# Second MLP product by one level of Strassen, with the sums of its weight blocks made by DMAs in HBM

## The chip, the cores and the metric

The kernel runs on one core of a Trainium2 chip. The metric is the device time of one execution in microseconds (us); lower is better. One execution was recorded by the hardware profiler; its rows are quoted below.

## What is computed

The kernel is a decoder layer for 512 tokens of width 1024: a gated merge of a convolution branch and an attention branch, a cross-attention to 256 memory tokens, a squared-ReLU MLP of width 4096, and a final norm. The change lies in the MLP:

```python
u = rms_norm(h, norm_mlp_g[l])                                      # [512, 1024]
h = h + jnp.square(jax.nn.relu(u @ w_mlp1[l])) @ w_mlp2[l]          # [1024, 4096], [4096, 1024]
return rms_norm(h, final_norm_g)
```

All is float32. The kernel makes each float32 product from three passes over operands that are split into a high and a low part.

## The kernel before

Activations lie feature-major, [feature, token]. A *unit* is one output tile: eight 128-row blocks of weights against 512 tokens, three passes each (`mm3`: high x high, high x low, low x high), so 24 matmuls of 128x512. The TensorE (PE) queue is in the order of emission; the queues of the other engines are put in order by a scheduler when the program is built, which may place an instruction earlier than the line that emits it if nothing holds it there.

Weights come from HBM as chunks of at most 1 MB into `raw` (two buffers, loads on SP's queue). `prep` splits a unit's part of a chunk: ScalarE (ACT) casts it into `wh`, and another engine subtracts to get `wl` (three buffers each). That other engine is `w_eng`: VectorE (DVE) for the first units, then GpSimd (POOL) from the third convolution tile on, through the input products, attention, merge and most of the cross-attention, and DVE again from `w_eng[0] = dve` just ahead of the MLP. `Pipe` emits a unit's split ahead of the products of the unit before it.

The MLP goes by halves of the hidden features. `m1_unit` makes one tile of the first product, `evac_m1` scales it by the row factors, squares and splits it into `hh` and `hl_`; then `m2_unit` multiplies the 16 tiles of the half by eight column tiles of `w_mlp2` and adds into the residual `ht`. That is 768 matmuls of 128x512 for the first product and 768 for the second. The last output tile goes by token halves, with the final norm of the first half beside the products of the second (`last_*`).

Of the kernel before, what the change touches and what calls it, by code (L numbers as in the profile page):

```python
# [23 lines left out]
P = 128  # L24
# [68 lines left out]
# gate chunks that come before the key/value latents  # L93
# [3 lines left out]
def _stream():  # L97
    """The weight chunks in the order of use: key, matrix, first row, row blocks, columns."""
# [34 lines left out]
    for h in range(2):  # L133
        for i in range(8):
            out.append((("m1", h, i), "w_mlp1", 0, 8, r(2048 * h + 256 * i, 256)))
        for i in range(8):
            out.append((("m2", h, i), "w_mlp2", 16 * h, 16, r(128 * i, 128)))
    return out


def _pack(arrays):
    """All weight chunks, each [partition, row block, column], one after the other."""
    parts = []
    for _, name, k0, kt, cols in _stream():
        w = arrays[name][0][k0 * P:(k0 + kt) * P]
# [20 lines left out]
def _body(tc, a):  # L166
# [30 lines left out]
    # ---------------------------------------------------------------- exact splits and products  # L197
# [8 lines left out]
    # PE issues in the order of emission; small products that wait for other engines are put off  # L206
    # by a number of ticks (a tick: three passes over 512 columns)
# [20 lines left out]
    def mm3(out, pairs, first=True, last=True):  # L228
        n = len(pairs)
        cols = out.shape[-1] / S  # L230
        for i, ((wh, wl), (ah, al)) in enumerate(pairs):
            pe.matmul(out, wh, ah, start=first and i == 0, stop=False)  # L232
            pe.matmul(out, wh, al, start=False, stop=False)  # L233
            pe.matmul(out, wl, ah, start=False, stop=last and i == n - 1)  # L234
            tick(cols)
# [11 lines left out]
    # ---------------------------------------------------------------- constants  # L247
# [31 lines left out]
    # ---------------------------------------------------------------- weight stream  # L279
    stream = _stream()  # L280
    ch, offs = {}, []
    o = 0
    for i, (key, _, _, kt, cols) in enumerate(stream):
        ch[key] = i
        offs.append(o)
        o += P * kt * len(cols)
    raws = {}
    issued = [0]
    RAW_BUFS = 2

    def raw(*key):
        ci = ch[key]
        while issued[0] < len(stream) and issued[0] < ci + RAW_BUFS:
# [4 lines left out]
            src = a["weights"][offs[i]:offs[i] + P * n].rearrange("(p n) -> p n", p=P)  # L298
# [27 lines left out]
    class Pipe:  # L326
        """splits the weights of one unit ahead of the unit before it."""
# [22 lines left out]
    # ================================================================ scopes of the first half  # L350
# [34 lines left out]
    # ---------------------------------------------------------------- x * g, split  # L385
    # the tables of the scalar engine and the clock of the PE array come up while the first loads run
# [34 lines left out]
    # ---------------------------------------------------------------- rotary tables  # L421
# [50 lines left out]
    # ---------------------------------------------------------------- background conv work  # L472
# [14 lines left out]
    def conv_gen():  # L487
        # two channel tiles in turn, so that no step waits for the one before it
# [16 lines left out]
    def layer_norm_in():  # L505
        # token-major
# [47 lines left out]
    # ---------------------------------------------------------------- w_in  # L554
# [41 lines left out]
    # first pair of channel tiles: both products follow the arriving row blocks of x  # L596
# [39 lines left out]
    # latent projections, token-major: [token, column]  # L636
# [94 lines left out]
    # ================================================================ MLA  # L731
# [148 lines left out]
    # ================================================================ merge and w_out  # L880
# [73 lines left out]
    class Norm:  # L954
        """h += psum; h * g, split; the sums of squares of h's rows."""

        def __init__(self, pl, gname, oh_, ol_):
# [18 lines left out]
        def sums(self):  # L976
            r = rstd_rows(self.acc, D)
            after(D_R2, lambda: self.bcast(r))
# [8 lines left out]
        def then(self, fn):  # L987
            """runs fn once the rows' factors are there."""
# [21 lines left out]
    for m in range(KD):  # L1010
        out_unit(m)
        if m == 2:
            mem_norm()
# [5 lines left out]
    # ================================================================ memory cross-attention  # L1019
# [97 lines left out]
    n2 = Norm(hgp, "norm_mlp_g", hgh, hgl)  # L1117
# [16 lines left out]
    pipe.ahead(lambda: prep(("m1", 0, 0)))  # L1134
    close(xa_cm, xm_cm)

    # ================================================================ MLP
    ml_cm, mlp = pool("mlp", side="right")
    hh = mlp.tile([P, 16, S], F32R, name="hh")
    hl_ = mlp.tile([P, 16, S], F32R, name="hl")  # L1140

    def evac_m1(b, m):
        t = mlp.tile([P, S], F32, tag="mz", name="mz", bufs=2)
        dve.scalar_tensor_tensor(t, b, 0.0, n2.rb, op0=ALU.max, op1=ALU.mult)  # L1144
        s = mlp.tile([P, S], F32, tag="ms", name="ms", bufs=2)
        act.activation(s, t, AF.Square)
        if m == 0:
            act.activation(warm, s[:, 0:1], AF.Sqrt)
        split(hh[:, m, :], hl_[:, m, :], s)

    def m1_unit(half, m):
        def main(hl):
            b = bank()
            mm3(b, hg_pairs(hl))
            n2.then(lambda: evac_m1(b, m))
        pipe.unit(lambda: prep(("m1", half, m // 2), c0=128 * (m % 2)), main)

    fin = mlp.tile([P, S], F32, name="fin")
    eps = mlp.tile([P, 1], F32, name="eps")
    gps.memset(eps, EPS)  # L1160
    mb_ = {}

    def m2_unit(half, m, q):
        def main(hl):
            if q == 0:
                mb_[0] = bank()
            b = mb_[0]
            mm3(b, [(lhs(hl, k), (hh[:, 8 * q + k, :], hl_[:, 8 * q + k, :])) for k in range(8)],
                first=q == 0, last=q == 1)
            if q == 1:  # L1170
                dve.tensor_tensor(ht[:, m, :], ht[:, m, :], b, op=ALU.add)
                if half == 1:
                    if m == 0:
                        act.activation(fin, ht[:, m, :], AF.Square)
                    else:
                        s = mlp.tile([P, S], F32, tag="ms", name="ms", bufs=2)
                        act.activation(s, ht[:, m, :], AF.Square)
                        dve.tensor_tensor(fin, fin, s, op=ALU.add)
                    act.activation(ht[:, m, :], ht[:, m, :], AF.Copy, scale=v_("final_norm_g", m))
        pipe.unit(lambda: prep(("m2", half, m), k0=8 * q, kt=8), main)  # L1180

    for half in range(2):
        for m in range(16):
            m1_unit(half, m)
        for m in range(KD - half):
            for q in range(2):
                m2_unit(half, m, q)
# [3 lines left out]
    m = KD - 1  # L1191
    lw = [prep(("m2", 1, m), k0=8 * q, kt=8) for q in range(2)]
    pipe.flush()
    HS = S // 2
    ydst = a["yT"].rearrange("(k p) t -> p k t", p=P)

    def last_mm(b, hf, i):
        """an eighth of the products of a token half."""
        sl = slice(hf * HS, hf * HS + HS)
        q, k0 = i // 4, 2 * (i % 4)  # L1200
        mm3(b[:, :HS], [(lhs(lw[q], k), (hh[:, 8 * q + k, sl], hl_[:, 8 * q + k, sl]))
                        for k in range(k0, k0 + 2)], first=i == 0, last=i == 7)

    def last_add(b, hf):
        """the sums of squares of a token half."""
        sl = slice(hf * HS, hf * HS + HS)
# [82 lines left out]
```

## Time and profile before

| what | value |
|---|---|
| time, median of 3 runs | 814.03 us (814.02 to 814.56) |
| span of the profiled execution, first to last instruction | 811.6 us |
| TensorE busy / weight load | 783.2 us (97%) / 647.3 us (80%) |
| VectorE / ScalarE / GpSimd busy | 495.9 us / 346.4 us / 158.6 us |
| mean granted TensorE clock | 0.989 |
| HBM read / written | 74.97 MB / 2.10 MB |

The profiled execution is read by its span; the median of the runs is 2.4 us above it, which is taken as what lies around the span. A busy PE means that a matmul is in flight, not that it is at its peak.

### The profile page before, as it was taken

How to read it: one execution, taken by the hardware profiler on the slowest of the kernel's cores; microseconds unless marked ns; L12 is line 12 of the kernel's file. 1: busy time of each engine (PE TensorE's matmuls, PEld its weight loads, DVE VectorE, ACT ScalarE, POOL GpSimd, SP SyncE). 2: the span in 40 equal slices, each digit the busy share in tenths (PEclk: the TensorE clock that was granted, in tenths of full speed). 3: DMA queues.
4: the chain of work that ended last, by engine and by line, in shares of the span. 5: the costliest groups of instructions: out<-in, count | busy, mean ns of one | idle time of the engine just before them, and what ended most of it. 6: DMA issues, size and time to landing. Idle time of an engine off the chain costs nothing.

```text
span 811.6 us, 9532 instructions
## 1 busy us (share of the span) xinstructions
PE 783.2 (97%) x3730; PEld 647.3 (80%) x3730; DVE 495.9 (61%) x781; ACT 346.4 (43%) x585; POOL 158.6 (20%) x92
## 2 busy tenths in 40 slices
PE   8799999999999998998999999999999999999995
PEld 4589788778788886888878888888888888888885
DVE  5898999734888869766787654443233444533333
ACT  7323334478666546343475354332212434432321
POOL 4444436322321304445320000000000000000001
PEclk9999999999999998999999999999999999999998
DMA  8213124122103242232321322222332222222203
GB/s 274 95 45 124 55 82 156 62 81 92 53 1 105 98 162 104 103 105 104 105 104 52 105 104 104 86 79 96 103 104 104 104 96 76 89 103 104 104 0 104
DMA packets 18492, 77.67 MB, mean 96 GB/s; under 512 B 1680, under 2 KB 7184, under 8 KB 11024
## 3 DMA queue, kind: packets, MB, share of 16 engines
q1 hardware_dynamic: 15120, 72.00, 25.6%
q10 hardware_dynamic: 3328, 5.07, 1.8%
q8 instruction: 29, 0.48, 0.2%
q14 instruction: 15, 0.12, 0.1%
HBM read 74.97 MB, written 2.10 MB: 95 GB/s over the span
## 4 chain that ended last, share of the span: by engine, by line
PE 75%; DVE 18%; ACT 3%; issue 3%; DMA 1%; SPq 0%; DVEq 0%; ACTq 0%
PE mm L234 23%; PE mm L232 23%; PE mm L233 23%; DVE cv L483 6%; DVE q L200 1%; DVE mt L906 1%; DVE rs_t L243 1%; DMA xr<-xT 1%; PE at L799 1%; DVE sg L710 1%; PE at L778 1%; PE at L780 1%; ACT wh L199 1%; PE at L781 0%; DVE mt L905 0%
## 5 line engine op out<-in xcount | busy, mean ns | idle before, releaser
L199 ACT CAST wh<-raw 128x1024 fp32r<-128x1024 f32 (+4 forms) x135 | 136.5, 1012 | 321.5 <-PE mm L233 279.7
L200 POOL TENSOR_TENSOR wl<-raw,wh 128x1024 fp32r<-128x1024 f32 (+4 forms) x65 | 144.6, 2227 | 255.2 <-ACT wh L199 248.1
L200 DVE TENSOR_TENSOR wl<-raw,wh 128x1024 fp32r<-128x1024 f32 x70 | 85.7, 1224 | 73.3 <-ACT wh L199 73.3
L232 PE MATMUL mm<-hgh,wh 128*128 128x512 f32 x288 | 113.0, 392 | 0.0
L234 PE MATMUL mm<-hgh,wl 128*128 128x512 f32 x288 | 112.8, 392 | 0.0
L233 PE MATMUL mm<-hgl,wh 128*128 128x512 f32 x288 | 112.6, 391 | 0.0
L232 PE MATMUL mm<-hh,wh 128*128 128x512 f32 (+1 forms) x272 | 102.6, 377 | 0.0
L233 PE MATMUL mm<-hl,wh 128*128 128x512 f32 (+1 forms) x272 | 102.4, 376 | 0.0
L234 PE MATMUL mm<-hh,wl 128*128 128x512 f32 (+1 forms) x272 | 102.4, 376 | 0.0
L483 DVE SCALAR_TENSOR_TENSOR cv<-zpad,vec,cv 128x512 f32<-128x512 f32 x116 | 80.0, 744 | 0.1
L1245 POOL TENSOR_TENSOR ht<-ht,rbf 128x256 f32<-128x256 f32 x4 | 2.9, 736 | 384.1 <-ACT rbf L1237 384.1
L232 PE MATMUL mm<-uh,wh 128*128 128x512 f32 x176 | 71.3, 405 | 1.8 <-DVE sg L710 1.8
L1144 DVE SCALAR_TENSOR_TENSOR mz<-mm,rb 128x512 f32<-128x512 f32 x32 | 22.0, 691 | 79.7 <-PE mm L234 78.7
L234 PE MATMUL mm<-uh,wl 128*128 128x512 f32 x176 | 69.8, 397 | 0.5 <-DVE wl L200 0.5
L233 PE MATMUL mm<-ul,wh 128*128 128x512 f32 x176 | 69.9, 397 | 0.0
L234 PEld LDWEIGHTS mm<-hgh,wl 128*128 128x128 f32 x288 | 54.3, 189 | 11.5
L233 PEld LDWEIGHTS mm<-hgl,wh 128*128 128x128 f32 x288 | 54.5, 189 | 11.2
L232 PEld LDWEIGHTS mm<-hgh,wh 128*128 128x128 f32 x288 | 54.5, 189 | 11.2
L234 PEld LDWEIGHTS mm<-hh,wl 128*128 128x128 f32 x272 | 51.2, 188 | 9.4
L232 PEld LDWEIGHTS mm<-hh,wh 128*128 128x128 f32 x272 | 51.2, 188 | 9.4
L233 PEld LDWEIGHTS mm<-hl,wh 128*128 128x128 f32 x272 | 51.2, 188 | 9.3
L232 PEld LDWEIGHTS mm<-uh,wh 128*128 128x128 f32 x176 | 33.3, 189 | 11.1 <-issue 3.8
(327 smaller groups left out, 1407.1 us busy)
## 6 DMA issues: line engine op xcount, KB each, us to landing
raw<-weights SPq DMA_DIRECT2D x58, 1024.0 KB, 4.8
raw<-weights SPq DMA_DIRECT2D x4, 768.0 KB, 4.2
xr<-xT SPq DMA_DIRECT2D x8, 256.0 KB, 6.2
raw<-weights SPq DMA_DIRECT2D x4, 512.0 KB, 5.1
ht<-xT ACTq DMA_DIRECT2D x1, 2048.0 KB, 9.4
raw<-weights SPq DMA_DIRECT2D x2, 576.0 KB, 3.4
mr<-memT ACTq DMA_DIRECT2D x1, 1024.0 KB, 5.8
mtok<-mem ACTq DMA_DIRECT2D x1, 1024.0 KB, 7.9
```

Source lines behind the costliest of these rows:

```text
L199: act.copy(hi, src)
L200: (eng or dve).tensor_tensor(lo, src, hi.bitcast(F32), op=ALU.subtract)
L232: pe.matmul(out, wh, ah, start=first and i == 0, stop=False)
L233: pe.matmul(out, wh, al, start=False, stop=False)
L234: pe.matmul(out, wl, ah, start=False, stop=last and i == n - 1)
L243: dve.scalar_tensor_tensor(t, dst, -0.5, dst, op0=ALU.mult, op1=ALU.mult)
L483: dve.scalar_tensor_tensor(run if w < CW - 1 else acc[:, c, :], zs, wcol, run, op0=ALU.mult, op1=ALU.add)
L710: dve.tensor_tensor(t, b, rbx, op=ALU.mult)
L778: pe.matmul(b[:, :n], q[:, 0, sl], k[:, 0, :n], start=True, stop=False)
L780: pe.matmul(b[:, :n], q[:, 0, sl], k[:, 1, :n], start=False, stop=False)
L799: pe.transpose(b[:, (t - k) * P:(t - k + 1) * P], ptok[h, t][:, k * P:(k + 1) * P], ident)
L1144: dve.scalar_tensor_tensor(t, b, 0.0, n2.rb, op0=ALU.max, op1=ALU.mult)
```

## The change

The hidden activations A (512 tokens by 4096) and the weights B (4096 by 1024) of the second product are each cut into two by two blocks, and the eight block products become seven (Strassen-Winograd). The operands are A11, S1, S2, S4, S3, A12, A22 against B11, X, Y, B22, V, B21, Z, with

- S1 = A21 - A22 (kept as `s3 - a22`), S2 = A11 - S1 with the signs as in the code, S3, S4 likewise: four subtractions on DVE for each pair of hidden tiles, beside the first product;
- X = B12 + B11, V = B12 + B22, Y = B11 + V, Z = B21 + Y: made in HBM, by 16 plain copies of 1 MB and 16 accumulating DMAs of 1 MB, all on POOL's queue (`b_sums`).

The second product becomes token-major: the activations' blocks are the stationary operand, 512 weight columns the moving one. It runs as 7 passes of 4 chunks; a chunk is one 1 MB load, one split of 128x1024 of activations (`split_h`) and two of weights (`split_w`), and 24 matmuls. A chunk needs a load of its own, so the product takes 28 loads of 1 MB where it took 16. The row factors are applied when the sums leave PSUM; the residual is transposed by PE beside the first product and written to HBM (`spill`), and read back for each output tile. The final norm is token-major.

```diff
+    def b_sums_gen():
+        ...
+        start = lambda c: [(("x", c), b12(c)), (("v", c), b12(c)), (("y", c), b11(c)), (("z", c), b21(c))]
+        adds = lambda c: [(("x", c), b11(c)), (("v", c), b22(c)), (("y", c), sums["v", c]),
+                          (("z", c), sums["y", c])]
+        for c in range(4):
+            for d, s_ in start(c):
+                gps.dma_start(out=sums[d], in_=s_)
+                yield
+            if c > 0:
+                for d, s_ in adds(c - 1):
+                    gps.dma_start(out=sums[d], in_=s_, accum_op=ALU.add, max_dma_last_dim=8192)
+                    yield
+        for d, s_ in adds(3):
+            gps.dma_start(out=sums[d], in_=s_, accum_op=ALU.add, max_dma_last_dim=8192)
+            yield
...
     for m in range(KD):
         out_unit(m)
+        b_sums(1)
...
+    def m1_unit(p, j):
+        ...
+            act.activation(r, b, AF.Relu)
+            for half in range(2):
+                dst = block((("a11", "a12"), ("s3", "a22"))[half][j], c)[:, i]
+                act.activation(dst, r[:, half * HT:(half + 1) * HT], AF.Square)
+            if j == 1 and p % 2 == 1:
+                dve.tensor_tensor(s1, s3, a22, op=ALU.subtract)
+                dve.tensor_tensor(s3, s3, a11, op=ALU.subtract)
+                dve.tensor_tensor(s2, a11, s1, op=ALU.subtract)
+                dve.tensor_tensor(s4, a12, s2, op=ALU.subtract)
+    def spill(m):
+        for t in range(NT):
+            pe.transpose(b[:, t * P:(t + 1) * P], ht[:, m, t * P:(t + 1) * P], ident)
+        act.copy(t_.rearrange("p t c -> p (t c)"), b)
+        act.dma_start(out=hsp[:, m * P:(m + 1) * P].rearrange("(t p) c -> p t c", p=P), in_=t_)
+    for p in range(16):
+        for j in range(2):
+            m1_unit(p, j)
+        if 1 <= p <= KD:
+            spill(p - 1)
+        b_sums(2)
...
+    def split_h(name, c):
+        pl = m2w.get("p", mlp)
+        hi = pl.tile([P, 4, HT], F32R, tag="hA", name="hA", bufs=2 if pl is not mlp else 1)
+        lo = pl.tile([P, 4, HT], F32R, tag="hB", name="hB", bufs=2 if pl is not mlp else 1)
+    PASSES = (("a11", "b11", "a", False), ("s1", "x", "c", False), ("s2", "y", "b", False),
+              ("s4", "b22", "c", True), ("s3", "v", "b", True), ("a12", "b21", "a", True),
+              ("a22", "z", "b", True))
+    for n in range(len(PASSES)):
+        for c in range(4):
+            pass_unit(n, c)
```

Where the scheduler puts the DMAs is not seen in the diff. The first place is the beginning of POOL's queue. The names: `wl` is the low part of a weight split, `xr` and `nacc` are the sums of squares of the input, `x_0_80` is the block sum X of chunk 0 in HBM, `weights` the packed weights; a DMA's shape is rows by elements. Before:

```order
L416 MEMSET cs_106 128x4
L200 ISA
L200 TENSOR_TENSOR wl_165<-raw_135,wh_164 128x256 [waits DMAHW3_49,Activation_49]
L200 TENSOR_TENSOR wl_165<-raw_135,wh_164 128x512 [waits DMAHW5_49,Activation_49]
L200 TENSOR_TENSOR wl_167<-raw_135,wh_166 128x512 [waits DMAHW0_49,Activation_49]
L200 TENSOR_TENSOR wl_167<-raw_135,wh_166 128x512 [waits DMAHW3_49,Activation_49]
L568 TENSOR_TENSOR xr_85<-xr_85 128x512 [waits Activation_49]
L568 TENSOR_TENSOR xr_85<-xr_85 128x512 [waits Activation_49,Pool_49] x2
L569 TENSOR_TENSOR nacc_86<-xr_85 128x512 [waits DVE_49,Pool_49]
```

Now:

```order
L474 MEMSET cs_124 128x4
L333 DMA x_0_80<-weights 16x16384
L333 DMA v_0_84<-weights 16x16384
L227 ISA
L227 TENSOR_TENSOR wl_183<-raw_153,wh_182 128x256 [waits DMAHW3_49,Activation_49]
L227 TENSOR_TENSOR wl_183<-raw_153,wh_182 128x512 [waits DMAHW5_49,Activation_49]
L227 TENSOR_TENSOR wl_185<-raw_153,wh_184 128x512 [waits DMAHW0_49,Activation_49]
L227 TENSOR_TENSOR wl_185<-raw_153,wh_184 128x512 [waits DMAHW3_49,Activation_49]
L626 TENSOR_TENSOR xr_103<-xr_103 128x512 [waits Activation_49]
L333 DMA y_0_88<-weights 16x16384
L626 TENSOR_TENSOR xr_103<-xr_103 128x512 [waits Activation_49,Pool_49]
L333 DMA z_0_92<-weights 16x16384
```

The copies that the code emits beside the merge product and the first MLP product stand at the very start of the program, two of them ahead of the first weight split.

The second place is farther down the same queue, in the gate products of the input stage, where the last chain of adds stands (Y of chunk 3 waits for V, Z for Y; DMASW names the landing of an earlier DMA of POOL's). Before:

```order
L694 TENSOR_TENSOR krr_110<-krt_109 128x4x16
L696 COPY krr_110<-krr_110 128x4x64 [waits Pool_49]
L200 TENSOR_TENSOR wl_1200<-raw_1082,wh_1199 128x1024 [waits DMAHW4_49,PE_49,Activation_49]
L200 TENSOR_TENSOR wl_1238<-raw_1082,wh_1237 128x1024 [waits PE_49,Activation_49]
L200 TENSOR_TENSOR wl_1278<-raw_1197,wh_1277 128x1024 [waits DMAHW5_49,PE_49,Activation_49]
```

Now:

```order
L340 DMA y_3_91<-v_3_87 128x2048 [waits DMASW6_49,DMASW4_49]
...
L227 TENSOR_TENSOR wl_1218<-raw_1100,wh_1217 128x1024 [waits DMAHW4_49,PE_49,Activation_49]
L754 COPY krr_128<-krr_128 128x4x64 [waits Pool_49]
L340 DMA z_3_95<-y_3_91 128x2048 [waits DMASW7_49,DMASW6_49]
L227 TENSOR_TENSOR wl_1256<-raw_1100,wh_1255 128x1024 [waits PE_49,Activation_49]
L227 TENSOR_TENSOR wl_1296<-raw_1215,wh_1295 128x1024 [waits DMAHW5_49,PE_49,Activation_49]
```

The last two accumulating DMAs, each waiting for the one before it in its chain, stand ahead of weight splits; all 32 DMAs stand ahead of the last row.

The third place is ScalarE at the start of the second product, where `hA` is the high part of a split of activations, `hres` a residual read back. Before, in the second product (`ht` is the residual):

```order
L199 CAST wh_5869<-raw_5805 128x1024 [waits DMAHW1_49,PE_49]
L1174 ACTIVATE fin_4111<-ht_2830 128x512 [waits DVE_49]
L1179 ACTIVATE ht_2830<-ht_2830,vec_69 128x512 [waits Activation_49]
L199 CAST wh_5902<-raw_5805 128x1024 [waits PE_49]
L199 CAST wh_5933<-raw_5867 128x1024 [waits DMAHW2_49,PE_49]
L1177 ACTIVATE ms_5898<-ht_2830 128x512 [waits DVE_49]
```

Now:

```order
L226 CAST hA_5453<-a11_2_4840 128x1024
L226 CAST wh_5414<-raw_5361 128x1024 [waits DVE_49,PE_49]
L226 CAST hA_5491<-hid3_5143 128x1024
L1329 DMA hres_6040<-hsp_4138 128x512 [waits DMAHW2_49,Activation_49]
L226 CAST hA_5404<-a11_1_4513 128x1024 [waits PE_49]
L226 CAST wh_5459<-raw_5408 128x1024 [waits DMAHW1_49,DVE_49,PE_49]
L1329 DMA hres_6047<-hsp_4138 128x512
L226 CAST wh_5463<-raw_5408 128x1024 [waits DVE_49,PE_49]
```

The split of the second chunk's activations (`a11_1`) waits for PE, since chunks 0 and 1 share one buffer; the later chunks have two.

## Rows read from the trace of the kernel before

**Rows 1.** Page, parts 1 to 3: span, busy time, 40 slices, the load queue.

```profile
span 811.6 us, 9532 instructions
PE 783.2 (97%) x3730; PEld 647.3 (80%) x3730; DVE 495.9 (61%) x781; ACT 346.4 (43%) x585; POOL 158.6 (20%) x92
...
GB/s 274 95 45 124 55 82 156 62 81 92 53 1 105 98 162 104 103 105 104 105 104 52 105 104 104 86 79 96 103 104 104 104 96 76 89 103 104 104 0 104
...
q1 hardware_dynamic: 15120, 72.00, 25.6%
```

**Rows 2.** Windows (stretch, us, busy of PE, PEld, DVE, ACT, POOL, clock, DMA share, GB/s).

```profile
0.00:10.00 10.00, 7.00 (x21) 3.09 (x21) 2.18 (x5) 5.29 (x9) 2.65 (x11) 1.00 0.77 227
10.00:20.00 10.00, 9.68 (x37) 6.47 (x38) 9.52 (x9) 8.87 (x16) 6.47 (x5) 1.00 0.99 317
375.00:380.00 5.00, 2.92 (x15) 2.18 (x14) 4.36 (x10) 1.55 (x3) 2.96 (x2) 1.00 0.54 210
380.00:385.00 5.00, 5.00 (x16) 3.94 (x16) 0.40 (x2) 0.73 (x2) 0.00 (x0) 0.66 0.00 0
500.00:550.00 50.00, 50.00 (x222) 41.39 (x222) 22.36 (x26) 19.54 (x26) 0.00 (x0) 1.00 0.30 105
0.00:142.80 142.80, 133.05 (x624) 108.05 (x625) 127.20 (x207) 55.71 (x92) 65.06 (x49) 0.99 0.35 118
```

**Rows 3.** Timeline, TensorE: first output product of the cross-attention; second MLP product.

```profile
428.11 0.39 PE L232 MATMUL mm<-xoh,wh 128*128 128x512 f32 x1
...
785.19 0.39 PE L232 MATMUL mm<-hh,wh 128*128 128x512 f32 x1
...
788.36 0.39 PE L234 MATMUL mm<-hh,wl 128*128 128x512 f32 x1
```

**Rows 4.** Timeline, POOL, ScalarE and TensorE: first instants, then 133 to 146 us.

```profile
1.40 0.10 POOL L416 MEMSET cs<- 128x4 f32 x1
...
133.51 0.39 PE L232 MATMUL mm<-uh,wh 128*128 128x512 f32 x1
133.53 1.05 ACT L199 CAST wh<-raw 128x1024 fp32r<-128x1024 f32 x1 [3.82 <-PE mm L233]
134.66 2.41 POOL L200 TENSOR_TENSOR wl<-raw,wh 128x1024 fp32r<-128x1024 f32 x1 [1.08 <-ACT wh L199]
...
145.59 0.47 PE L232 MATMUL mm<-uh,wh 128*128 128x512 f32 x1 [0.73 <-DVE sg L710]
```

**Rows 5.** DMA issues (KB each, median us to landing); loads' landing, 440 to 790 us.

```profile
raw<-weights SPq DMA_DIRECT2D x58, 1024.0 KB, 4.8
yT<-ht SPq DMA_DIRECT2D x4, 256.0 KB, 2.5
DMA to landing us min/median/max: 4.6/4.8/5.9
```

**Rows 6.** Groups by form (busy us, mean ns of one).

```profile
L199 ACT CAST wh<-raw 128x1024 fp32r<-128x1024 f32 x119 | 124.9, 1051 | 294.7 <-PE mm L233 261.2 <-issue 20.4 <-PE mm L234 13.0
L200 DVE TENSOR_TENSOR wl<-raw,wh 128x1024 fp32r<-128x1024 f32 x70 | 85.7, 1224 | 73.3 <-ACT wh L199 73.3
L1171 DVE TENSOR_TENSOR ht<-ht,mm 128x512 f32<-128x512 f32 x15 | 10.3, 687 | 50.3 <-PE mm L234 50.3
```

**Rows 7.** Timeline, TensorE: eight transposes of 128x128 and what follows.

```profile
405.28 1.03 PE L1084 MATMUL at<-kon,xp 128*128 128x128 f32 x8
406.07 0.48 PE L232 MATMUL mm<-wh,mh 128*128 128x512 f32 x1
```

**Rows 8.** Timeline of the end, after the last product.

```profile
801.64 0.28 PE L234 MATMUL mm<-hh,wl 128*128 128x256 f32 x1
...
803.72 0.26 ACT L1226 ACTIVATE rs_q<-at,eps 128x2 f32<-128x2 f32 x1 [0.89 <-DVE rv L1225]
804.01 0.17 DVE L1227 RECIPROCAL rr<-rs_q 128x2 f32<-128x2 f32 x1 [0.33 <-ACT rs_q L1226]
...
807.42 0.47 DVE L1241 SCALAR_TENSOR_TENSOR ht<-ht,vec,at 128x256 f32<-128x256 f32 x1
```

More of the change, by code (lines that the diff above doesn't have):

```diff
@@ L226, in _body, with mm3 @@
     bg = lambda w: None
-    def mm3(out, pairs, first=True, last=True):
+    def mm3(out, pairs, first=True, last=True, again=False):
         n = len(pairs)
@@ L1154, in main @@
             mm3(b, hg_pairs(hl))
[L1155 to L1180, printed above, removed]
@@ L1204, in last_add @@
-    def last_add(b, hf):
-        sl = slice(hf * HS, hf * HS + HS)
-        dve.tensor_tensor(ht[:, m, sl], ht[:, m, sl], b[:, :HS], op=ALU.add)
-        s = mlp.tile([P, HS], F32, tag="msl", name="msl", bufs=2)
-        act.activation(s, ht[:, m, sl], AF.Square)
-        return s
-    sb = {}
-    def last_sums(hf, sq, last):
-        if not last:
-            sb[hf] = bank("at")
-        for t in range(2):
-            pe.matmul(sb[hf][:, t:t + 1], sq[:, t * P:(t + 1) * P], ones1, start=not last and t == 0,
-                      stop=last and t == 1)
@@ new lines, in split_h, with split_w @@
+    def split_h(name, c):
+        pl = m2w.get("p", mlp)
+        hi = pl.tile([P, 4, HT], F32R, tag="hA", name="hA", bufs=2 if pl is not mlp else 1)
+        lo = pl.tile([P, 4, HT], F32R, tag="hB", name="hB", bufs=2 if pl is not mlp else 1)
+        src = block(name, c)
+        if name == "a22":
+            split_scaled(hi, lo, src, -1.0)
+        else:
+            split(hi, lo, src)
+        return hi, lo
+    def split_w(src):
+        out = []
+        for u in range(2):
+            w = whl4(2, S)
+            split(w[0], w[1], src[:, 2 * u:2 * u + 2, :])
+            out.append(w)
+        return out
@@ new lines, in chunk, with big @@
+    def chunk(out, h, w, c, again=False, by_tile=False):
+        order = [(k, t) for t in range(2) for k in range(4)] if by_tile else \
+                [(k, t) for k in range(4) for t in range(2)]
+        for k, t in order:
+            sl = slice(t * P, (t + 1) * P)
+            mm3(out[t], [((h[0][:, k, sl], h[1][:, k, sl]), lhs(w[k // 2], k % 2, 0, S))],
+                first=not again and c == 0 and k == 0, last=c == 3 and k == 3, again=again)
+    keep, acc_ = {}, {}
+    free_ = []
+    def big(name, bufs=2):
+        return m2w["p"].tile([P, S], F32, tag=name, name=name, bufs=bufs)
@@ new lines, in done_r5, with done_q6, done_c12 @@
+    def done_r5():
+        for t in range(2):
+            keep["s5", t] = big("s5")
+            act.copy(keep["s5", t], acc_["c"][t])
+    def done_q6():
+        for t in range(2):
+            keep["w2", t] = big("w2")
+            dve.tensor_tensor(keep["w2", t], acc_["b"][t], keep["s1", t], op=ALU.subtract)
+    def done_c12():
+        yy = mlp.tile([P, 2, S], F32, tag="hA", name="y12", bufs=1)
+        for t in range(2):
+            y = yy[:, t]
+            stt(y, keep["w2", t], r2(t), residual(t, 1))
+            stt(y, acc_["c"][t], r2(t), y)
+            y_done(t, 1, y)
+            keep["y", t, 1] = y
@@ new lines, in pass_unit, with prep_, main @@
+    def pass_unit(n, c):
+        aname, bname, bk, again = PASSES[n]
+        def prep_():
+            return split_h(aname, c), split_w(raw("m2", n, c))
+        def main(hw):
+            if not again and c == 0:
+                acc_[bk] = [bank("at" if bk == "b" else "mm") for _ in range(2)]
+            last = n == len(PASSES) - 1 and c == 3
+            chunk(acc_[bk], *hw, c, again, by_tile=last)
+            if n == 0 and c == 0:
+                late_pools()
+            if c == 3:
+                if last:
+                    for t in range(2):
+                        done_c21(t)
+                else:
+                    DONE[n]()
+        pipe.unit(prep_, main)
```

250 lines of the change are left out of this document (166 added, 84 removed).

## The prediction

> **What bounds the kernel now.** The page comes first: TensorE is busy for 783.2 of 811.6 us [rows 1]. In the stretch around 500 us it is busy for 50.00 of 50.00 us at the full granted clock of 2.4 GHz, while DVE and ACT work 22 and 20 us and the DMA engines 30% [rows 2]. The timeline shows the pace there: fifteen matmuls of 128x512 stand from 785.19 to 788.36 us, so 3.17 / 14 = 0.2264 us each, and a unit of 24 takes 5.43 us [rows 3]. So in the MLP a matmul taken away is 0.2264 us, as long as splits and loads keep up. The second place to look is where the change puts its DMAs, in the first 143 us of POOL's queue. There POOL makes the low parts of the weights, and PE waits for these if POOL is held.
>
> **Savings and costs in the MLP, step by step.**
>
> *Fewer products.* 7 passes of 4 chunks of 24 matmuls are 672 against 768: 96 x 0.2264 = 21.7 us off. Both kinds are 128x512.
>
> *Transposes of the residual.* 32 of 128x128. Eight take 406.07 - 405.28 = 0.79 us, and the switch back costs about 0.1 us [rows 7]: 32 x 0.099 + 8 x 0.1 = 4.0 us on. Their copies (ACT) and DMAs hide under the products, beside which ACT works 20 of 50 us [rows 2]. The bounds are 3.2 and 5 us.
>
> *Small products gone.* The broadcast of the row factors, the sums of squares and the token halves go. The cross-attention's output product begins at 428.11 us and has 96 matmuls, so the MLP begins near 449.9 us [rows 3]; its last product ends at 801.9 us [rows 8]. Of these 352.0 us 1536 x 0.2264 = 347.8 are products. Of the other 4.2 us about 1.2 stay: 3.0 us off.
>
> *Splits in the second product.* A chunk needs three casts of 1.05 us on ACT and three subtractions of 1.22 us on DVE [rows 6], 3.2 and 3.7 us of the 5.43. Hidden, but DVE has only 1.7 us to spare. Where it isn't hidden: the second chunk shares its activation buffer with the first, so its cast and subtraction follow the end of the first chunk, 1.05 + 1.22 = 2.3 us. At the end of the fifth pass six DVE operations of 0.69 us [rows 6] stand ahead of the next split: 4.1 + 1.2, about 0.3 us late with the semaphores. At the end of the sixth pass some 16 operations stand between the splits, two of which wait for a square root on ACT; worked through in their order with 0.69, 1.22 and 0.17 us [rows 6, 8], they make PE wait twice, 1.5 and 1.4 us. Sum 5.5 us on. If the scheduler's order hides all, it is 0; if each longer wait also lowers the clock it is more: after an idle of 2.1 us within 375 to 380 us the next 5 us ran at 0.66, 1.7 us lost [rows 2], which makes 9 us the upper bound.
>
> *Loads.* A chunk of 1 MB every 5.43 us against one in two units. Two buffers give a load about 6.4 us: two chunks last 10.9 us, and the splits hold a buffer for some 4.4. Loads land in 4.8 us, 5.9 at most [rows 5]. Hidden, and 0.5 us for each 1 us over 6.4 in each of 28 chunks if not.
>
> *The end.* Now 9.7 us lie between the last product's end and the end of the span [rows 1, 8]. After the change: an addition 0.7, a square 0.65, six small operations and a root of about 0.2 each, a multiplication 0.75 and a store of 2.5 [rows 5, 6, 8], with the way out 7.7 us: 2.0 off.
>
> Sum of the MLP: -21.7 + 4.0 - 3.0 + 5.5 - 2.0 = -17.2 us.
>
> **The block sums, which decide.** The order shows all 32 DMAs of 1 MB hoisted to the input stage, between POOL's weight splits. POOL's queue is in order, so a DMA that waits for the landing of an earlier one holds the splits behind it, then ACT's buffers, then PE. The last such row is Z of chunk 3, which waits for Y of chunk 3: by then 16 copies and 15 adds must have run. The split behind it starts at 134.66 us and takes 2.41 us; its unit starts at 145.59 us and uses the low part in its third matmul, near 146.1 us [rows 4]. So POOL may be 9.0 us late, until 143.6 us.
>
> What the DMA engines must do by then: the load queue moved 72.00 MB in 25.6% of 811.6 us, 346 GB/s while at work [rows 1], so 1 MB (1.049 million bytes) is 3.03 us of all engines. Until 142.8 us the loads already take 35%, 50.0 us [rows 2]. The copies are 16 x 3.03 = 48.5 us. The trace has no accumulating DMA, nor one from HBM to HBM. Nothing lets an add be less than a copy, 3.03. If it reads source and destination through the same engine before it writes, it is two reads, 6.06; if reading, reading and writing follow each other, 9.1 (a copy then 6.06). I take 3.03 for a copy and 6.06 for an add, since each load shows reading and writing side by side, and an add has one reading more: 15 x 6.06 = 90.9 us. POOL is free at 1.5 us [rows 4], and landing takes 4.8 - 3.03 = 1.8 us beyond the transfer, issue some 0.3: 1.5 + 50.0 + 48.5 + 90.9 + 2.1 = 193.0 us, 49.4 us after the moment when PE must wait. Earlier chains (Y of chunk 1 and 2) already hold POOL in the same way; this is their sum and not on top. A bound below is 15 x 3.03: 147.5 us, 3.9 us late; a bound above 95 us late, or 143 with the dearer copies.
>
> The Trainium skill (Collectives: The Full Stack, section "The bandwidth ceiling: the fold count and why AG ≠ RS ≠ AR") says of such adds that the arithmetic is free and that two source reads on one ring halve the rate of a copy, which is the ratio taken here. Its figure of 31 GB/s for an engine's copies between HBM buffers would give, as an estimate, 2.1 us for a copy, 4.2 us for an add, POOL 7 us late and 803 us in all, with the cheap rival below; no run here shows it.
>
> *The start.* X and V of chunk 0 are copied while the first loads arrive, with the engines 77% and 99% taken [rows 2]: 6.1 us of work put between them delays the first products by 2 to 6 us, 4 taken. It is inside the 49.4 us, since PE that starts later is due later by as much; it counts alone only if POOL never holds PE.
>
> **Sum.** 811.6 - 17.2 + 49.4 = 843.8 us of span, with 2.4 us around it 846.2: I predict 846 us.
>
> **The rivals.**
>
> *The adds are cheap (faster).* The place is the same row of POOL's queue, Z of chunk 3. The delay eats the whole saving when it is 17.2 us, so at (143.6 + 17.2 - 1.5 - 50.0 - 48.5 - 2.1) / 15 = 3.9 us an add. Below that the kernel is faster: at 3.03 us, with the start, 814.03 - 17.2 + 4 = 801 us. For it: 317 GB/s over 10 us [rows 2] shows engines near their rate with loads alone, and in HBM two reads need not cost two transfers. Against it: an add moves three times 1 MB through 16 engines. Chance 0.21.
>
> *The adds are dearer (slower still).* At 9.1 us 95 us late, 892 us; with copies of 6.06 us 940 us. For it: the destination must be read before it is written, and both ends lie in HBM, which no row shows. Chance 0.27.
>
> *The second product is held by its loads.* 28 MB in 152 us, with a landing of 7 us: 28 x 0.3 = 8 us on whatever the sums make; with cheap adds 809, near no change. Landings of 4.6 to 5.9 us speak against it [rows 5]. Chance 0.07.
>
> **How the numbers follow.** The forecast (adds at two reads, delay of 20 to 75 us, 817 to 872 us) has 0.45. A measurement of this kernel can tell about 0.2%, 1.6 us, from no change. Faster is the cheap case, 0.21; no change is a delay of 16 to 19 us, or cheap adds with slow loads, 0.05; slower the rest, 0.74. The range reaches from the cheap case's middle, 802, to adds at three transfers, 895; about 0.1 is left out on either side.
>
> **What would show it.** In the trace after: POOL's DMAs in the first 200 us; POOL idle ahead of `wl` with a DMA as releaser; PE idle in the input stage for tens of us, with `wl` or `wh` behind it; the MLP from its first product to its end 352 - 15 = 337 us. The forecast is wrong if PE's idle time in the first 250 us hardly grows (adds cheap), if the wait is at loads of `raw` and not at POOL, or if the second product's 672 matmuls take much more than 158 us.

## The result and the profile after

The changed kernel takes 827.19 us (median of 4 runs, 826.74 to 830.54) where the kernel before takes 814.02: a ratio of 1.0169, 95% interval 1.0151 to 1.0188. It is slower by 13.2 us; 32 were forecast. The page of the kernel after, parts 1 to 3, beside [rows 1]:

```profile
span 825.0 us, 9536 instructions
...
PE 769.2 (93%) x3594; PEld 632.5 (77%) x3594; DVE 537.8 (65%) x808; ACT 400.4 (49%) x681; POOL 175.1 (21%) x120
...
PE   5889974889999999899899999999999999999995
...
DMA  8899999971220214421422123322322355555564
...
q1 hardware_dynamic: 16048, 85.37, 28.9%
q0 software_dynamic: 2816, 33.56, 15.3%
```

PE falls short in the first nine slices (186 us), hardly later; in the first eight of them the DMA engines are busy for 80% or more. The window of these DMAs has a DMA share of 0.96, where [rows 2] has 0.35 until 142.8 us:

```profile
0.00:172.50 172.50, 139.50 (x631) 115.65 (x632) 134.06 (x215) 56.56 (x96) 78.88 (x79) 0.91 0.96 280
```

The waits of the kernel after (us in total, times, longest); the three of PE are from its first 250 us:

```profile
PE at L262 <- POOL wl L227: 11.0, 1, 11.0
PE mm L263 <- POOL wl L227: 9.8, 4, 4.5
PE mm L669 <- ACT uh L230: 7.3, 1, 7.3
...
ACT wh L226 <- DMA raw<-weights: 53.8, 11, 8.8
POOL y L337 <- DMA v<-weights: 30.3, 3, 19.0
POOL z L337 <- DMA y<-v: 14.0, 3, 5.9
POOL z L340 <- DMA y<-v: 7.8, 1, 7.8
```

POOL stands for 52.1 us at adds into Y and Z that wait for a landing, and PE for 20.8 us at the weight splits behind them. POOL's timeline shows the two side by side, and the last row is the split that [rows 4] has at 134.66 us:

```profile
141.76 0.81 POOL L337 DMA_DIRECT2D y<-v  x1 [19.00 <-DMA v<-weights]
142.31 1.68 POOL L227 TENSOR_TENSOR wl<-raw,wh 128x576 fp32r<-128x576 f32 x1
...
152.07 0.83 POOL L337 DMA_DIRECT2D z<-y  x1 [5.88 <-DMA y<-v]
...
172.49 0.82 POOL L340 DMA_DIRECT2D z<-y  x1 [7.85 <-DMA y<-v]
173.06 7.29 POOL L227 TENSOR_TENSOR wl<-raw,wh 128x1024 fp32r<-128x1024 f32 x3
```

How late the input stage is can be read from a later split of the same kind, when the sums are over. Before and after:

```profile
192.37 1.87 POOL L200 TENSOR_TENSOR wl<-raw,wh 128x768 fp32r<-128x768 f32 x1 [8.04 <-ACT wh L199]
```

```profile
223.00 1.85 POOL L227 TENSOR_TENSOR wl<-raw,wh 128x768 fp32r<-128x768 f32 x1 [7.78 <-ACT wh L226]
```

It is 30.6 us late. PE's waits behind POOL are 20.8 us of that and the late start is 6. The rest is mostly granted clock: it fell after the waits of 11.00, 2.29 and 2.18 us that ended at 144.04, 155.32 and 175.73 us, as the clock column (third from the end) of the windows behind them shows:

```profile
144.00:150.00 6.00, 5.96 (x30) 5.96 (x30) 0.00 (x0) 0.54 (x1) 2.20 (x2) 0.62 1.01 212
155.00:160.00 5.00, 4.68 (x14) 3.76 (x14) 5.00 (x8) 1.05 (x1) 3.67 (x5) 0.66 1.06 239
175.00:180.00 5.00, 4.27 (x12) 3.37 (x13) 4.93 (x9) 0.64 (x1) 5.00 (x3) 0.66 1.02 236
```

Then TensorE's timeline gives the MLP: the first product from 478.57 us, the second from 657.57, its second chunk with two waits, the pace of the later chunks, and the last product.

```profile
478.57 0.39 PE L261 MATMUL mm<-hgh,wh 128*128 128x512 f32 x1
...
657.57 0.39 PE L261 MATMUL mm<-wh,hA 128*128 128x512 f32 x1
...
664.08 0.50 PE L261 MATMUL mm<-wh,hA 128*128 128x512 f32 x1 [0.91 <-ACT hA L226]
...
665.96 0.50 PE L263 MATMUL mm<-wh,hB 128*128 128x512 f32 x1 [1.14 <-DVE hB L227]
...
749.09 0.40 PE L261 MATMUL at<-wh,hA 128*128 128x512 f32 x1
...
757.50 0.39 PE L261 MATMUL at<-xh,hA 128*128 128x512 f32 x1
...
760.24 0.40 PE L261 MATMUL at<-wh,hA 128*128 128x512 f32 x1
...
816.31 0.39 PE L263 MATMUL at<-xh,hB 128*128 128x512 f32 x1
```

The 36 matmuls from 749.09 us take 8.41 us, 0.2336 each; the 12 from 757.50 take 2.74, 0.228; the first 24, before the waits, keep to 0.2265.

From its first product to the end of the span the MLP takes 825.0 - 478.57 = 346.4 us; before it began at 449.87 us, so 361.7. That is 15.3 us less, where 17.2 were predicted. The span adds up: 811.6 + 30.6 - 1.9 (the stretch from that split to the MLP, 255.6 us instead of 257.5) - 15.3 = 825.0 us.

### The profile page after: what moved, and what is told of

Same layout as the page of the kernel before. It is cut to its first block, busy times and chain, and to the rows that moved or that the text cites. A ratio compares the mean times of both kernels' runs of the same rounds, so it can differ in the third digit from the quotient of the medians.

```text
span 825.0 us, 9536 instructions
## 1 busy us (share of the span) xinstructions
PE 769.2 (93%) x3594; PEld 632.5 (77%) x3594; DVE 537.8 (65%) x808; ACT 400.4 (49%) x681; POOL 175.1 (21%) x120
## 3 DMA queue, kind: packets, MB, share of 16 engines
q1 hardware_dynamic: 16048, 85.37, 28.9%
q0 software_dynamic: 2816, 33.56, 15.3%
HBM read 124.78 MB, written 37.75 MB: 197 GB/s over the span
## 4 chain that ended last, share of the span: by engine, by line
PE 66%; DVE 12%; issue 8%; DMA 7%; ACT 4%; POOL 3%; SPq 0%; POOLq 0%; DVEq 0%; ACTq 0%
PE mm L263 18%; PE mm L262 18%; PE mm L261 18%; DMA v<-weights 3%; PE at L262 2%; PE at L263 2%; PE at L261 2%; POOL wl L227 2%; DMA raw<-weights 2%; DMA xr<-xT 1%; DVE q L227 1%; DVE mt L964 1%; ACT wh L226 1%; PE at L857 1%; DVE wl L227 1%
## 5 line engine op out<-in xcount | busy, mean ns | idle before, releaser
L226 ACT CAST wh<-raw 128x1024 fp32r<-128x1024 f32 (+4 forms) x146 | 147.5, 1013 | 278.8 <-PE mm L262 148.8
L227 POOL TENSOR_TENSOR wl<-raw,wh 128x1024 fp32r<-128x1024 f32 (+4 forms) x65 | 148.5, 2300 | 211.6 <-ACT wh L226 208.4
L227 DVE TENSOR_TENSOR wl<-raw,wh 128x1024 fp32r<-128x1024 f32 x81 | 98.9, 1223 | 132.0 <-ACT wh L226 132.0
L262 PEld LDWEIGHTS mm<-hgl,wh 128*128 128x128 f32 x288 | 54.1, 188 | 10.9
L261 PEld LDWEIGHTS mm<-hgh,wh 128*128 128x128 f32 x288 | 54.1, 188 | 10.9
L263 PEld LDWEIGHTS mm<-uh,wl 128*128 128x128 f32 x176 | 34.5, 196 | 22.6 <-POOL wl L227 11.5
L263 PE MATMUL mm<-wh,hB 128*128 128x512 f32 x100 | 39.6, 396 | 1.1 <-DVE hB L227 1.1
L261 PE MATMUL mm<-wh,hA 128*128 128x512 f32 x100 | 39.6, 396 | 0.9 <-ACT hA L226 0.9
L262 PEld LDWEIGHTS mm<-ul,wh 128*128 128x128 f32 x176 | 34.7, 197 | 7.1
L262 PE MATMUL mm<-wl,hA 128*128 128x512 f32 x100 | 39.5, 395 | 0.0
L262 PE MATMUL at<-wl,hA 128*128 128x512 f32 x72 | 28.6, 397 | 0.3 <-DVE wl L227 0.3
L261 PE MATMUL mm<-mgh,wh 128*128 128x512 f32 x64 | 26.0, 406 | 3.1 <-ACT mgh L226 3.1
## 6 DMA issues: line engine op xcount, KB each, us to landing
x<-weights POOLq DMA_DIRECT2D x4, 1024.0 KB, 18.7
```

Of the source, the lines that this page charges most:

```text
L226: act.copy(hi, src)
L227: (eng or dve).tensor_tensor(lo, src, hi.bitcast(F32), op=ALU.subtract)
L261: pe.matmul(out, wh, ah, start=first and i == 0, stop=False, **kw)
L262: pe.matmul(out, wh, al, start=False, stop=False, **kw)
```

## The experiments

The theory after this first reading: the MLP gains what it should, POOL is held by the DMA engines' work as predicted, and only the price of a transfer was too high. Its rivals: the chain of landings decides and not the work; slower loads do it and not POOL; a copy is cheaper still and an add costs 6.06.

All twelve kernels are read by the same marks: the time, its ratio to the kernel before on the same chip, the start of the split of 192.37 us, the MLP's first product, and from there to the end of the span.

| kernel | time, us | ratio (95%) | split | MLP from | MLP |
|---|---|---|---|---|---|
| before | 814.02 | | 192.37 | 449.87 | 361.7 |
| after | 827.19 | 1.0169 (1.0151 to 1.0188) | 223.00 | 478.57 | 346.4 |
| 1 no sums | 796.98 | 0.9815 (0.9785 to 0.9845) | 190.69 | 446.51 | 346.3 |
| 2 copies | 813.35 | 0.9996 (0.9969 to 1.0022) | 206.89 | 460.50 | 348.2 |
| 3 held at their place | 800.53 | 0.9850 (0.9833 to 0.9868) | 191.86 | 449.89 | 348.1 |
| 4 Y, Z late | 806.30 | 0.9923 (0.9896 to 0.9950) | 199.75 | 458.79 | 348.0 |
| 5 copies, rows of 8 KB | 810.11 | 0.9955 (0.9939 to 0.9971) | 205.68 | 461.53 | 346.6 |
| 6 later start | 824.98 | 1.0134 (1.0115 to 1.0153) | 219.80 | 477.80 | 348.1 |
| 7 as 3, 32 bytes up | 795.49 | 0.9790 (0.9763 to 0.9816) | 191.25 | 445.29 | 348.2 |
| 8 as 7, own buffer | 795.64 | 0.9773 (0.9752 to 0.9794) | 191.74 | 449.87 | 343.6 |
| 9 eight more copies | 845.85 | 1.0398 (1.0363 to 1.0432) | 239.59 | 495.45 | 346.6 |
| 10 as 8, 16 KB up | 795.24 | 0.9765 (0.9739 to 0.9792) | 191.51 | 449.60 | 343.7 |

Between the split and the MLP these programs have the same products and splits, but 254 to 259 us pass. PE has two waits there, of 3.1 us (at `mgh`) and 2.3 us (at `rr`); the granted clock differs (over 20 us around the second it is 0.91 in experiment 3 and 1.00 in experiment 5), and experiments 2 and 7 lack the second wait. So single microseconds are read from the other columns and not from the time.

**1. No sums.**

```diff
-            src = sums[stream[i][1], stream[i][2]] if stream[i][1] in SUMS else chunk_hbm(i)
+            src = chunk_hbm(ch["b12", stream[i][2]]) if stream[i][1] in SUMS else chunk_hbm(i)
...
     def b_sums(n):
-        for _ in range(n):
-            next(b_gen, None)
+        pass
```

> Leaves out all 32 block-sum DMAs; the second product's chunks that read X, Y, V and Z read plain blocks of the weights in their place, so 28 loads of 1 MB stay and the output is not the layer's. Theory: the input stage lost 30.3 us in the kernel after to these DMAs and nothing else did, so the time is 827.2 - 30.3 = 796.9 us, which is 17.1 under the kernel before. Rival A: part of the 30.3 us comes from elsewhere (other instruction order in the input stage); then it ends above 800. Rival B: the DMAs cost nothing in the input stage and the second product loses instead; then it ends near 827.

Measured 796.98 us (four runs, 794.63 to 798.84), with the split 1.7 us earlier than before and an MLP as in the kernel after. The whole loss is the DMAs', all of it in the input stage; both rivals fall.

**2. Copies in place of adds.**

```diff
-                    gps.dma_start(out=sums[d], in_=s_, accum_op=ALU.add, max_dma_last_dim=8192)
+                    gps.dma_start(out=sums[d], in_=s_)
```

> The 16 accumulating DMAs become plain copies with the same source, target, place and waits, so X, Y, V, Z are not sums and the output is not the layer's. Theory: the engines' work decides. With 3.03 us for each of 31 DMAs the last wait ends at 1.5 + 50.0 + 31 x 3.03 + 2.1 = 147.5 us, 4 us late, at most the 6 us of the start: about 803 us, and POOL's DMA queue takes 32 x 3.03 = 97 us of engine time where the kernel after has 126, which makes an add (126.2 - 16 x 3.03) / 16 = 4.9 us. Rival A: a copy costs less, 1.9 us, and an add 6.06 as predicted; the time is 803 again, but the queue takes only 60 us. Rival B: the chain of landings decides and not the engines' work; the chain is as long as before, so the time stays above 815 us.

POOL's queue on the page of the copies kernel (packets, MB, share of 16 engines), span 808.7 us:

```profile
q0 software_dynamic: 1024, 33.56, 10.9%
```

10.9% of 808.7 is 88.1 us for 32 copies: 2.75 us each, and in the kernel after an add is (126.2 - 44.1) / 16 = 5.13 us. Rival A falls (60 us). The time is not the theory's: 813.35 us, the median of ten runs from 807.90 to 822.22 (812.16 without the slowest, which the ratio leaves out), so rival B (above 815) isn't clearly out by the time. The split is 14.5 us late. By the sum the last wait ends at 1.5 + 50.0 + 31 x 2.75 + 2.1 = 138.9 us and holds nobody; in the trace the last add's stand-in is issued at 149.11 us, still no wait of PE names POOL's `wl`, and yet more is lost than the start. PE waits twice for `sg`, an operation of DVE, 2.69 us until 105.92 and 3.45 us until 158.12 us (1.8 us in all in the kernel before). Ahead of the second wait:

```profile
149.68 4.74 POOL L227 TENSOR_TENSOR wl<-raw,wh 128x1024 fp32r<-128x1024 f32 x2
149.91 4.54 DVE L274 SCALAR_TENSOR_TENSOR rr<-rs_t,rr 128x4 f32<-128x4 f32 x1
...
158.12 0.77 PE L261 MATMUL mm<-uh,wh 128*128 128x512 f32 x1 [3.45 <-DVE sg L768]
```

POOL, held for 3.78 us ahead of that stand-in, makes two splits back to back, and an operation of DVE that took 0.15 us at 147.78 takes 4.54 beside them; at 98.50 us another took 5.21 beside two splits. The granted clock is 0.61 in 160 to 165 us, behind the second wait.

**3. Held at their place.**

```diff
-                gps.dma_start(out=sums[d], in_=s_)
+                tc.keep_in_program_order(gps.dma_start(out=sums[d], in_=s_))
```

The same for the adds: the scheduler may not place such a DMA ahead of the POOL instruction emitted before it.

> Nothing left out. Each block-sum DMA is held behind the POOL instruction that the code emits before it: 8 copies stand in the merge product and 24 DMAs back to back at the start of the first MLP product, where POOL has no splits. Theory: the input stage gets its 30.3 us back and nothing waits for POOL; 797 to 800 us. Rival: the 24 DMAs take the engines for about 95 us while the first product's loads of 1 MB are due every 10.9 us; a load that lands in 12 us, as under the same contention in the input stage of the kernel after, still fits two buffers, but one of 19 us, as the adds took there, does not: up to 8 loads late by some 3 us each, 805 to 822 us.

Measured 800.53 us, 13.5 less than before and half a microsecond above the theory's range; the split is on time again. Windows of the first MLP product, in which the 24 DMAs run, and the loads' landing there (KB, median us):

```profile
440.00:460.00 20.00, 20.00 (x94) 16.68 (x93) 16.01 (x29) 12.30 (x19) 3.63 (x6) 1.00 1.03 310
480.00:500.00 20.00, 20.00 (x92) 16.52 (x91) 7.52 (x8) 9.27 (x18) 4.53 (x7) 1.00 1.05 322
```

```profile
raw<-weights SPq DMA_DIRECT2D x11, 1024.0 KB, 7.9
```

The engines are as full as in the input stage, a load lands in 7.9 us instead of 4.8 [rows 5], and PE works 20.00 of 20.00 us: a load is due every 10.9 us and nothing waits for POOL there. The rival falls. The 32 DMAs take 16.2% of 798.0 us here, 129.3 us, so at 2.75 us a copy an add beside the first MLP product is 5.3 us.

**4. Only the adds into Y and Z held.** The copies and the adds into X and V stay in the input stage; each of the other eight follows a small POOL copy of a result of the first product. Those that stay are emitted three to a tile of the merge product.

```diff
-        b_sums(1)
+        b_sums(3)
...
-        b_sums(2)
+        tc.keep_in_program_order(gps.tensor_copy(mark[:, p:p + 1], block("a11", p // 4)[:, p % 4, 0:1]))
+        b_sums(1)
```

> Nothing left out. The 16 copies and the 8 adds into X and V stay in the input stage; the 8 adds into Y and Z, the only ones that wait for another sum, are held in the first MLP product. Theory: POOL is no longer held for 52 us by landings; left are the late start (5.8 us) and the two or three waits for a copy's landing: 802 to 808 us. Rival: not POOL's queue but the slower loads (12.1 us to landing instead of 4.8) cost the time; 24 of 32 DMAs still run beside the loads, so two thirds of the 30.3 us stay: 815 to 820 us.

Measured 806.30 us, the split 7.4 us late. The queue's share until 200 us is 42.5%, 85 us of engine time, as much as in the copies kernel, and ACT waits no shorter for loads (24.9 us there):

```profile
ACT wh L226 <- DMA raw<-weights: 28.7, 8, 7.0
```

So the same work without the chain of waits on POOL costs 7.4 us (the start, where PE waits for the first loads, is 6 of them), with it 14.5 (copies); slower loads cost little beyond the start, and the rival falls. PE's wait for `sg` is 0.7 us here, where the copies kernel had 6.1: what the chain cost there passed through DVE and the clock. With the dear adds, work and chain together cost 30.6.

**5. Copies with the adds' rows.**

```diff
-                    gps.dma_start(out=sums[d], in_=s_, accum_op=ALU.add, max_dma_last_dim=8192)
+                    gps.dma_start(out=sums[d], in_=s_, max_dma_last_dim=8192)
```

> As the copies kernel (no sums are formed, the output is not the layer's), but the 16 copies that stand for the adds keep the adds' rows of 8 KB where the copies kernel had 64 KB. Theory: what makes an add dearer than a copy is the second read; the POOL queue's engine time stays near the 88 us of the copies kernel and the span near its 808.7. Rival: the smaller rows make it dearer; the engine time goes to the 126 us of the kernel after and the span towards its 825.

```profile
q0 software_dynamic: 2816, 33.56, 10.9%
```

The packets are those of the kernel after, the time is that of copies (10.9% of 808.1 us): what makes an add dear is the accumulating, not the row. That it is the second read, as the theory says, isn't shown: the pages count 124.78 MB read from HBM in this kernel and in the kernel after alike.

**6. Later start.**

The gate is POOL's first addition to the squares of the input; each block-sum DMA stays behind it.

```diff
+    def held(ins):
+        if gate:
+            tc.add_manual_dep(ins.ins, gate[0].ins.name, mybir.DependencyInfo(
+                mybir.DependencyClass.NoSync, mybir.DependencyReason.DATA), reason="start")
```

> Nothing left out. The kernel after with all its block-sum DMAs held behind POOL's first addition to the squares of the input (some 16 us instead of 1.4), otherwise in the same place. Theory, the prediction's step: the late start of PE lies inside the last wait, since the engines' work ends no earlier; PE starts 5.8 us sooner, but the last add into Z still is issued near 172 to 178 us: 825 to 832 us. Rival: the start adds to the rest: 827.2 - 5.8 = 821.4 us, and the last add into Z is issued near 166.

PE's first splits are on time, the last add into Z is issued at 179.86 us instead of 172.49, and the time is 824.98 us (four runs, 823.31 to 827.80): 5.8 us won at the start became 2.2. The time lies between the theory's range and the rival's, the last add comes later than either said, and the run can't decide between them: the DMAs are not in the same place. The gate moved the last add into Z two splits down POOL's queue, ahead of the one that began at 147.99 us in the kernel before instead of 134.66, so it was issued 7.4 us later but also stood ahead of a split that comes 13.3 us later. Whether an earlier start brings the last add forward stays open.

**7. 32 bytes up.** The second product's pool gets a pad of 32 bytes ahead of its activations.

> Nothing left out. The kernel with the DMAs held at their place, and every tile of the second product's pool moved up by 32 bytes, so that the split activations there and the weight splits lie at the same offset within 64 bytes. In the kernel after, the matmuls of the chunks from the third on took 0.2333 us where weights in wh and wl met activations of that pool, and 0.2266 where xh and xl of the same pool did. Theory: the differing offset is the cause; all matmuls take 0.2266 and 504 x 0.0067 = 3.4 us go: 797.1 us. Rival: the cause is the region or the writers of wh and wl; the pace stays at 0.2333 and the time at 800.5.

Its MLP takes 348.2 us, as without the pad, and the pace stays: 36 with `wh` and `wl` take 8.40 us, 12 with `xh` and `xl` 2.74. The theory falls. The 5 us in the time lie ahead of the MLP (it begins at 445.29 us with the split at the same place), where the edit changes nothing. There PE waits for `rr` in experiment 3:

```profile
375.76 2.37 POOL L227 TENSOR_TENSOR wl<-raw,wh 128x1024 fp32r<-128x1024 f32 x1 [0.41 <-ACT wh L226]
375.80 2.34 DVE L274 SCALAR_TENSOR_TENSOR rr<-rs_t,rr 128x4 f32<-128x4 f32 x1
...
379.00 1.12 PE L295 MATMUL at<-kon,rr 128*128 128x128 f32 x4 [2.28 <-DVE rr L274]
```

and not in experiment 7:

```profile
375.69 0.16 DVE L274 SCALAR_TENSOR_TENSOR rr<-rs_t,rr 128x4 f32<-128x4 f32 x1
375.91 0.65 PE L295 MATMUL at<-kon,rr 128*128 128x128 f32 x4
...
376.67 2.40 POOL L227 TENSOR_TENSOR wl<-raw,wh 128x1024 fp32r<-128x1024 f32 x1 [2.23 <-ACT wh L226]
```

POOL's split, behind a load that landed later, begins after DVE's operation and not beside it, so that takes 0.16 us instead of 2.34; the wait is gone, and so is the lower clock behind it (0.77 in 380 to 385 us in experiment 3, 1.00 here). That the pad did this isn't shown: one of its four runs took 799.43 us, the others 795.10 to 795.52.

**8. A buffer of its own for the second chunk.**

```diff
-        pl = m2w.get("p", mlp)
+        pl = m2w.get("p", hop if (name, c) == ("a11", 1) else mlp)
...
-            if n == 0 and c == 0:
+            if n == 0 and c == 1:
                 late_pools()
```

> Nothing left out. The kernel of the run before this one, and the second chunk's activations split into a buffer of their own in place of the one that the first chunk still reads. Theory: the two waits of PE at the second chunk, 2.4 us over the pace, go, and with them the 1.6 us that the lower granted clock cost after them in some executions: 793 to 795 us. Rival: the splits of that chunk are late anyway, since ACT and DVE still have the last tiles of the first product before them; the waits only move and the time stays within 1 us of the run before.

The MLP takes 343.6 us instead of 348.2, since PE no longer waits at the second chunk: the expected 4.0 us and 0.6 more. By the trace the rival falls. The time, 795.64, is 0.6 us above the theory's range and within the rival's 1 us of the run before, whose stretch ahead of the MLP was 4.6 us shorter; against experiment 3, with the MLP from 449.89 us as here from 449.87, it is 4.9 us less. By the MLP it is the best version with run 10, 2.3% under the kernel before; by the time alone runs 7, 8 and 10 are equal.

**9. Eight more copies.**

```diff
+                if d[0] in "xv":
+                    gps.dma_start(out=extra[2 * c + "xv".index(d[0])], in_=s_)
```

> Nothing left out; the kernel after with eight more copies of 1 MB into blocks of HBM that nothing reads and nothing waits for, beside the copies of X and V. The order of POOL's queue moves with them: the last add into Z now stands ahead of the split that began at 166.1 us in the kernel before (at 134.7 in the kernel after), so its due time is 175 instead of 143.6 us. Theory: the engines' work decides. By then they have 56.4 us of loads (35% of 142.8 and 20% of 32.2 us), 24 copies at 2.75 and 15 adds at 5.13 us: 1.5 + 56.4 + 66.0 + 77.0 + 2.1 = 203.0 us, 28 us late; the time stays within 5 us of 827. Rival: the chain of landings decides; it is as long as in the kernel after and has 31 us more room, so PE is hardly late at its end: 800 to 812 us.

```profile
213.85 0.81 POOL L343 DMA_DIRECT2D z<-y  x1 [10.28 <-PE at L574]
```

The row puts the wait down to PE; Y, for which this add waits too, was issued at 202.76 us, and such adds land in 9.3 us here. The time is 845.85 us, above both ranges: 22 us of engine time that nothing waits for cost 18.7 us, so the chain of landings alone, which had 31 us more room, doesn't decide. The queue's 17.6% of 842.0 us is 148.2 us, and 24 x 2.75 + 16 x 5.13 is 148.1: the prices hold. The last add is issued 10.9 us after the sum of the work (203.0), so the theory's sum is too short: the engines have a share of 0.91 over the first 215 us, 19 us idle, where the kernel after has 7 us idle of 172.5. That POOL, itself held, issues the next DMA late and the engines run dry meanwhile is the likely reason; no run tests it.

**10. 16 KB up.** As run 8 without the pad, four other buffers allocated ahead of the activations.

> Nothing left out. As the run with a buffer of its own for the second chunk, without the move by 32 bytes; the split activations of the second product's pool lie 16 KB farther up in a partition (from 68,608 bytes instead of 52,224). Theory: the pace of 0.2333 us is a matter of where stationary and moving operand lie; the first two chunks, with activations far off at 97 and 205 KB, take 0.2266 us with the same wh and wl, so the pace is 0.2266 for all and the MLP takes 343.6 - 3.4 = 340.2 us from its first product to the end of the span. Rival: it is something else that begins with the third or fourth chunk (what ACT, DVE or the DMAs do beside it): the pace stays, 343.6 us.

The MLP takes 343.7 us and the pace stays. The theory falls again; what makes the pace is open.

## Why the prediction was right in direction and wrong in size

**The step that failed** is the price of the transfers: "I take 3.03 for a copy and 6.06 for an add". They measured 2.75 and 5.13 us. Put into the same sum, 1.5 + 50.0 + 16 x 2.75 + 15 x 5.13 + 2.1 = 174.6 us, 31.0 us after the due moment of 143.6, where 49.4 were forecast; the trace has the last add into Z at 172.49 us, 28.9 us after it, and the stage 30.6 us late; the other 1.7 us are the lower clock behind the last wait (0.66 over 5 us). With this the span would have come to 811.6 - 17.2 + 31.0 = 825.4 us, and it is 825.0. That it fits so closely is partly luck: the loads, 50.0 us in the sum, took 44.3 (25.7% of 172.5 us), the engines were idle for 7 us that the sum doesn't have, and the MLP's missing 1.9 us are made up by the 1.9 us between split and MLP. The 3.03 was read from a queue that loads SBUF, with small loads among its packets; a copy from HBM to HBM is another transfer. That this is why it was too high was only argued. Nor does any run show that a load reads and writes side by side, from which the 6.06 was taken.

The Trainium skill (Collectives: The Full Stack, section "The bandwidth ceiling: the fold count and why AG ≠ RS ≠ AR") gives, for the adds of a collective, the second read as the reason of a halved rate. Here an add takes 5.13 / 2.75 = 1.87 times a copy. The trace agrees with the rate; the reason no run shows. Its 31 GB/s for an engine doesn't show, 65.5 KB in 2.75 us are 23.8, and the 803 us that the prediction estimated from it add up to 804.

**The mechanism was right.** The DMAs stand where the order had them, the engines are full until the last wait (0.96), POOL's queue holds the splits, and PE waits for `wl`. Experiment 3 takes only the place away, and the split is back at 191.86 us; of the time 26.7 us come back, since the stretch ahead of the MLP and the MLP itself were 2.5 and 1.7 us longer there.

**The start** was put at 2 to 6 us and inside the delay: the first splits are 5.8 to 6.1 us late. In the trace the 28.9 us at the last add and the 1.7 us of clock make up the 30.6 without them, as predicted; whether that add would have come sooner with an earlier start experiment 6 can't tell, since it moved the add as well.

**The MLP**, -17.2 forecast and -15.3 measured. First product: 657.57 - 478.57 = 179.0 us, of which 173.9 are products; the other 5.1 are the transposes and what was left of the small products, for which 4.0 and 1.2 were summed. Second product: 816.7 - 657.57 = 159.1 us, where 152.1 + 5.5 were summed. The wait at the second chunk came as forecast (1.07 + 1.31 = 2.4 us beyond the pace; 2.3), those at the ends of the fifth and sixth pass, 3.2 us, did not (0.3), and behind the second chunk 468 matmuls with `wh` and `wl` ran at 0.2334 us on average and 156 with `xh` and `xl` at 0.2286 instead of 0.2264, 3.6 us that nothing of before had shown. The end: 8.3 us against 7.7. The loads are hidden: they land in 4.8 to 4.9 us in the second product, and PE waits for none. From the first product to the last it is 338.1 us, where the prediction's sign was 337.

**The rivals.** Dearer adds and a second product held by its loads fell. Cheap adds were put at 801 us at the price of a copy, with a point of decision at 3.9 us an add. Experiments 2 and 5 are that case, and gave 813 and 810. The reasoning was that only the start counts once the last wait holds nobody. In the copies kernel the earlier waits in POOL's queue cost some 7 us more, by way of DVE operations beside POOL's closed-up splits and of the clock, which the prediction put at nothing; so the true point lies near the price of a copy.

## What to carry to other kernels

A DMA that nothing holds back is issued where the scheduler finds it ready, not where the code has it: when an engine computes as well as issues, look at what stands behind each DMA that waits for a landing, and hold such DMAs at a place where that engine has nothing else to do. That one edit made a change that cost 1.7% one that gains 1.5%. Work for the DMA engines is summed in their own time, each kind of transfer at a price from its own kind. The sum leaves out the engines' idle time, here 7 to 19 us; in two other kernels the last add came 10 and 11 us after it. When the largest wait is gone, the next ones count, and they may stand on another engine.

## What the runs showed of the hardware

An accumulating DMA from HBM to HBM took 5.13 us of 16 engines for 1 MB in the kernel after (5.3 in experiment 3); a copy took 2.75, with rows of 8 KB as with rows of 64.

Three operations of DVE on 128x4 that take 0.15 us by themselves took 2.34, 4.54 and 5.21 us beside splits on POOL (experiments 3 and 2).

The same two waits of PE at the second chunk were followed by a lower granted clock in some kernels and not in others. After them the kernel of experiment 3 has 1.7 us more, with eight matmuls 0.43 us apart instead of 0.23, the lower level of 1.2 GHz:

```profile
635.00:640.00 5.00, 3.46 (x10) 2.48 (x11) 4.49 (x4) 1.30 (x2) 0.00 (x0) 0.83 0.70 252
640.00:645.00 5.00, 5.00 (x20) 4.01 (x19) 2.36 (x2) 2.80 (x3) 0.00 (x0) 0.83 0.10 31
```

The kernel after, with a granted clock of 1.00 over the same stretch, has none of it: that is the difference of MLPs of 346.4 and 348.1 us.

Matmuls of one shape ran at two paces at the full granted clock: 0.2334 us with `wh` and `wl` moving against activations of the second product's pool, 0.2286 with `xh` and `xl` against the same, and 0.2265 with `wh` and `wl` in the first chunk. Neither 32 bytes nor 16 KB of address changed it; the cause stays open.
